# Gate and up of a SwiGLU layer as seven products of quarters, with DMAs that add in place

## The chip, the core and the metric

The kernel runs on one core of a Trainium2 chip. TensorE (PE) multiplies, VectorE (DVE) and ScalarE (ACT) work on tiles in on-chip memory, GpSimd (POOL) does some of the same work and issues DMAs, and SyncE (SP) issues most DMAs. The metric is the device time of one execution in microseconds (us).

## The reference

One step of a hybrid decoder layer on 512 prompt tokens and 8 sample tokens: parallel mLSTM and retention heads, cross attention into 256 memory tokens, and a dense SwiGLU layer. All that the change concerns is the last:

```python
D_MODEL = 1024; D_FF = 2816
...
hf = rmsnorm(x, g_ffn)
x = x + (jax.nn.silu(hf @ w_gate) * (hf @ w_up)) @ w_down
...
y = rmsnorm(x, g_final)
```

The arithmetic is fp32.

## The kernel before

**Data.** Activations lie transposed: 128 of the 1024 features on the partitions, eight such rows (`KB` = 8), and the N = 520 tokens in the free dimension, in two halves of H2 = 260. `X` holds the residual stream. An fp32 product is made of three matmuls of a rounded type: each operand is split into a high part (an ACT copy into the rounded type) and a low part (what is left, a DVE subtraction), and high·high, high·low and low·high are summed in PSUM. `split` (L179) does that for activations, `wload` (L188) for weights: SP loads 512 KB into one of three `wraw` tiles (L191), ACT casts (L195), DVE or at times POOL makes the low part (L196), in two pairs of tiles `whi`, `wlo`. `Weights` (L119) hands out the weights in a fixed order, one ahead of its use. `mm_k` (L206, matmul at L210) issues the six matmuls (128x128 by 128x260) of one row, `proj` (L234) the eight rows of one output block, 48 matmuls into a pair of PSUM banks, of which there are two (`ps2`).

**The stage.** The SwiGLU layer begins when the last rows of `A`, the split input times its gain, and the row factors `r_bc` (the norm's 1/rms, L262 to L265) are made. The 2816 hidden features are `FB` = 22 blocks of 128. For each block the loop at L1114 runs 48 matmuls for gate (`pfg`), takes them out of PSUM times `r_bc` (DVE, L1120), applies Silu (ACT, L1121), runs 48 matmuls for up (`pfu`), takes them out (DVE, L1124), multiplies (POOL, L1125) and splits the product into `FF` (L1126). Then come the eight output blocks of w_down (L1130 on), 22 rows of `FF` each, and the last of them in two halves of the tokens with the final norm and the stores behind (`finish`, L1143).

**Order.** The kernel is written against a tile framework (`tile.TileContext` with `schedule_with_timeline_sim=True`): a scheduler fixes ahead of time the order of the instructions on each engine, and each engine runs its list in order. Pools of rotating buffers (`bufs`) decide when a load may start.

Of the kernel before, what the change touches and what calls it, by code (L numbers as in the profile page):

```python
# [23 lines left out]
P = 128  # L24
# [66 lines left out]
def weight_order():  # L91
# [27 lines left out]
class Weights:  # L119


    def __init__(self, load, order):
        self.load, self.todo, self.ready, self.at = load, list(enumerate(order)), [], 0

    def get(self, ahead=1):
        while self.todo and len(self.ready) <= ahead:
            index, (_, _, nk, _, ncol) = self.todo.pop(0)
            self.ready.append(self.load(index, self.at, nk, ncol, len(self.todo) < 3))
            self.at += P * nk * ncol
        return self.ready.pop(0)  # L130
# [3 lines left out]
def decoder_step(ctx: ExitStack, tc: tile.TileContext, i: dict, o: list):  # L134
# [7 lines left out]
    apool_cm = tc.tile_pool(name="apool", bufs=1, side="right")  # L142
    apool = apool_cm.__enter__()
    bpool_cm = tc.tile_pool(name="bpool", bufs=1)
    bpool = bpool_cm.__enter__()
# [33 lines left out]
    def split(hi, lo, src, scale=None):  # L179
# [4 lines left out]
        else:  # L184
            act.activation(hi, src, AF.Copy, scale=scale)
            dve.scalar_tensor_tensor(lo, src, scale, hi.bitcast(F32), ALU.mult, ALU.subtract)

    def wload(index, at, nk, ncol, kept):  # L188
        n = nk * ncol
        raw = wp.tile([P, KB * P], F32, tag="wraw", name="wraw", bufs=3)  # L190
        sp.dma_start(raw[:, :n], i["weights"][at : at + P * n].rearrange("(p n) -> p n", p=P))  # L191
# [41 lines left out]

    def proj(x, name, order=range(KB)):  # L234
        hi, lo = W.get()
        ps = ps2(name)
# [61 lines left out]
    pool.memset(gw.bitcast(F32), 0.0)  # L298
    bg = main.tile([P, 8], F32, name="bg")
    m0 = main.tile([NS, 4], F32, name="m0")  # L300
    pool.dma_start(bg, i["b_gate"].broadcast_to([P, 8]))
# [808 lines left out]
    cx.close()  # L1110
    bpool_cm.__exit__(None, None, None)


    fx = ExitStack()  # L1114
    fp = fx.enter_context(tc.tile_pool(name="fp", bufs=2))
    FF = fp.tile([P, 2, FB, N], F32R, name="FF", bufs=1)
    for f in range(FB):
        ps = proj(A, "pfg")
        g = fp.tile([P, N], F32, tag="fg", name="fg")
        dve.tensor_tensor(halves(g), ps[:, :, :H2], r_h, ALU.mult)  # L1120
        act.activation(g, g, AF.Silu)  # L1121
        ps = proj(A, "pfu")
        u = fp.tile([P, N], F32, tag="fu", name="fu")
# [3 lines left out]
    apool_cm.__exit__(None, None, None)  # L1127
    tc.keep_in_program_order(act.preload_act_table_set(LOG_EXP))

    yx = ExitStack()  # L1130
    yp = yx.enter_context(tc.tile_pool(name="yp", bufs=4, side="right"))
    for ob in range(KB - 1):
        ps = ps2("pfd")
        for k0 in range(0, FB, KB):
            hi, lo = W.get()
            for k in range(min(KB, FB - k0)):
                mm_k(ps, hi, lo, FF, k, k0 + k, k0 + k == 0, k0 + k == FB - 1)
        xb = X[:, ob]
        dve.tensor_tensor(halves(xb), halves(xb), ps[:, :, :H2], ALU.add)
        square(yp, ob)  # L1140
        act.activation(xb, xb, AF.Copy, scale=vec[:, ob, V_GO : V_GO + 1])

    xb = X[:, KB - 1]  # L1143
    chunks = []
    def finish(ts, n, ps):
# [3 lines left out]
        dve.tensor_tensor(xb[:, ts], xb[:, ts], ps, ALU.add)  # L1149
        sq7 = yp.tile([P, n], F32, name="sq7")  # L1150
# [4 lines left out]
        r = yp.tile([P, n], F32, name="r")  # L1155
        rsqrt_rows(yp, r, pn)
# [90 lines left out]
```

## Time and profile before

| | before |
|---|---|
| median of 3 runs | 896.25 us (893.82 to 897.25) |
| the profiled execution's own time | 898.87 us |
| its span in the profile | 897.10 us |
| gate and up, first to last matmul | 499.9 to 756.65 us |
| w_down up to its last block | 756.65 to 867.55 us |
| PE busy | 863.6 us |
| DVE busy | 573.1 us |
| ACT busy | 349.7 us |
| POOL busy | 212.0 us |

The profile is of one execution. A busy time is that of an engine over the whole span. The chain of waits follows the work that ended last back from the end, at each step to what released it. In the timeline a bracket gives the idle time of the engine before an instruction and what ended it. Windows give the busy time of PE, its weight load, DVE, ACT and POOL in a stretch with the number of instructions in parentheses, then the granted TensorE clock (1.00 is full), the share of time that the DMA engines were busy, and GB/s. A DMA has two times: its issue on a queue and its landing.

### The profile page before, as it was taken

How to read it: one execution, taken by the hardware profiler on the slowest of the kernel's cores; microseconds unless marked ns; L12 is line 12 of the kernel's file. 1: busy time of each engine (PE TensorE's matmuls, PEld its weight loads, DVE VectorE, ACT ScalarE, POOL GpSimd, SP SyncE). 2: the span in 40 equal slices, each digit the busy share in tenths (PEclk: the TensorE clock that was granted, in tenths of full speed). 3: DMA queues.
4: the chain of work that ended last, by engine and by line, in shares of the span. 5: the costliest groups of instructions: out<-in, count | busy, mean ns of one | idle time of the engine just before them, and what ended most of it. 6: DMA issues, size and time to landing. Idle time of an engine off the chain costs nothing.

```text
span 897.1 us, 17057 instructions
## 1 busy us (share of the span) xinstructions
PE 863.6 (96%) x6923; PEld 846.3 (94%) x6923; DVE 573.1 (64%) x1251; ACT 349.7 (39%) x658; POOL 212.0 (24%) x210
## 2 busy tenths in 40 slices
PE   6999989999999999999999899999999999999994
PEld 5989989999999999889999899999999999999994
DVE  5899998877886678867888844444444444232224
ACT  5445525444545344365443432222222223222221
POOL 5554432221025201423323211111111111010011
PEclk9999989999999999999999999999999999999998
DMA  8323323333345347775663233333233332223213
GB/s 266 96 95 122 102 76 118 121 102 122 107 142 202 95 142 232 250 251 159 212 215 115 71 95 94 94 88 85 90 93 95 95 94 81 91 90 104 91 42 95
DMA packets 34599, 110.56 MB, mean 123 GB/s; under 512 B 4000, under 2 KB 8480, under 8 KB 34264
## 3 DMA queue, kind: packets, MB, share of 16 engines
q1 hardware_dynamic: 28752, 96.06, 34.8%
q0 software_dynamic: 3616, 12.34, 3.9%
q10 hardware_dynamic: 2152, 1.08, 0.5%
q8 instruction: 54, 0.88, 0.4%
q14 instruction: 25, 0.20, 0.1%
HBM read 100.38 MB, written 9.07 MB: 122 GB/s over the span
## 4 chain that ended last, share of the span: by engine, by line
PE 74%; DVE 15%; DMA 5%; issue 2%; ACT 2%; POOL 1%; SPq 0%; DVEq 0%; ACTq 0%; POOLq 0%
PE pfg L210 14%; PE pfu L210 14%; PE pfd L210 12%; PE pcq L210 4%; PE pwc L210 3%; PE ppl L210 3%; PE pgt L210 3%; PE pwo L210 3%; PE prp L210 3%; DVE cv L505 2%; DVE wlo L196 2%; PE pcv L210 1%; PE pfd L1171 1%; DMA Ss<-in_state_S_dram 1%; DMA X<-in_x_dram 1%
## 5 line engine op out<-in xcount | busy, mean ns | idle before, releaser
L195 ACT CAST whi<-wraw 128x1024 fp32r<-128x1024 f32 (+1 forms) x140 | 144.9, 1036 | 318.1 <-issue 113.5
L196 DVE TENSOR_TENSOR wlo<-wraw,whi 128x1024 fp32r<-128x1024 f32 (+1 forms) x121 | 176.8, 1462 | 81.2 <-ACT whi L195 79.1
L210 PE MATMUL pfg<-A,whi 128*128 128x260 f32 x704 | 114.3, 284 | 0.4 <-DVE fg L1120 0.4
L210 PE MATMUL pfu<-A,whi 128*128 128x260 f32 x704 | 113.6, 283 | 0.0
L210 PE MATMUL pfd<-FF,whi 128*128 128x260 f32 x616 | 99.0, 282 | 0.0
L210 PEld LDWEIGHTS pfg<-A,whi 128*128 128x128 f32 x704 | 97.8, 191 | 0.6 <-issue 0.6
L210 PEld LDWEIGHTS pfu<-A,whi 128*128 128x128 f32 x704 | 96.8, 188 | 0.1
L210 PEld LDWEIGHTS pfd<-FF,whi 128*128 128x128 f32 x616 | 84.6, 188 | 0.0
L1125 POOL TENSOR_TENSOR fu<-fu,fg 128x520 f32<-128x520 f32 x22 | 28.8, 1309 | 227.0 <-ACT whi L195 203.1
L210 PE MATMUL pfg<-A,wlo 128*128 128x260 f32 x352 | 71.4, 285 | 0.0
L210 PE MATMUL pfu<-A,wlo 128*128 128x260 f32 x352 | 71.1, 283 | 0.0
L1124 DVE TENSOR_TENSOR fu<-pfu,r_bc 128x520 f32<-128x520 f32 x22 | 15.4, 699 | 76.7 <-PE pfu L210 76.7
L210 PE MATMUL pfd<-FF,wlo 128*128 128x260 f32 x308 | 61.9, 282 | 0.0
L196 POOL TENSOR_TENSOR wlo<-wraw,whi 128x1024 fp32r<-128x1024 f32 x19 | 45.5, 2397 | 66.9 <-ACT whi L195 61.8
L289 POOL TENSOR_TENSOR ssq<-ssq,sq 128x520 f32<-128x520 f32 x18 | 29.3, 1630 | 125.6 <-ACT sq L288 120.4
L210 PEld LDWEIGHTS pfg<-A,wlo 128*128 128x128 f32 x352 | 54.8, 190 | 0.0
L210 PEld LDWEIGHTS pfu<-A,wlo 128*128 128x128 f32 x352 | 54.3, 188 | 0.0
L210 PE MATMUL pwc<-B,whi 128*128 128x260 f32 x256 | 43.9, 287 | 4.0 <-DVE X L278 3.0
L210 PE MATMUL ppl<-A,whi 128*128 128x260 f32 x256 | 47.0, 297 | 0.6 <-DVE up L497 0.6
L210 PEld LDWEIGHTS pfd<-FF,wlo 128*128 128x128 f32 x308 | 47.4, 188 | 0.0
L210 PE MATMUL pcv<-A,whi 128*128 128x260 f32 x256 | 45.8, 295 | 0.6 <-ACT whi L195 0.6
L210 PE MATMUL prp<-A,whi 128*128 128x260 f32 x256 | 44.3, 289 | 0.0
(382 smaller groups left out, 1972.3 us busy)
## 6 DMA issues: line engine op xcount, KB each, us to landing
wraw<-in_weights_dram SPq DMA_DIRECT2D x132, 512.0 KB, 3.6
kv<-in_cache_k_dram SPq DMA_DIRECT2D x16, 512.0 KB, 4.4
kv<-in_cache_v_dram SPq DMA_DIRECT2D x16, 512.0 KB, 4.5
wraw<-in_weights_dram SPq DMA_DIRECT2D x8, 384.0 KB, 3.1
X<-in_x_dram SPq DMA_DIRECT2D x2, 1040.0 KB, 6.2
Cs<-in_state_C_dram POOLq DMA_DIRECT2D x4, 512.0 KB, 5.1
out_dram<-Cs POOLq DMA_DIRECT2D x4, 512.0 KB, 3.2
Ss<-in_state_S_dram POOLq DMA_DIRECT2D x4, 512.0 KB, 4.4
```

What stands on the lines that cost most here:

```text
L195: act.copy(hi[:, :n], raw[:, :n])
L196: (pool if index in LO_ON_POOL else dve).tensor_tensor(lo[:, :n], raw[:, :n], hi[:, :n].bitcast(F32), ALU.subtract)
L210: pe.matmul(ps[:m, a, :H2], w[:, k, c0 : c0 + m], x[:, s, xk, a * H2 : (a + 1) * H2], start=first and w is hi and s == 0, stop=last and w ...
L289: (dve if ob == KB - 1 else pool).tensor_tensor(ssq, ssq, s, ALU.add)
L505: dve.scalar_tensor_tensor(cv[:, :LO], up[:, j : j + LO], wc(j), cv[:, :LO], ALU.mult, ALU.add)
L1124: dve.tensor_tensor(halves(u), ps[:, :, :H2], r_h, ALU.mult)
L1125: pool.tensor_tensor(u, u, g, ALU.mult)
L1171: pe.matmul(ps, w[:, k], FF[:, s, k0 + k, ts], start=k0 + k == 0 and w is hi and s == 0, stop=k0 + k == FB - 1 and w is lo,)
```

## The change

Gate and up of a hidden block are together a product of a 2x2 array of weight quarters (a11, a12: the two halves of a gate tile along the 1024 features; a21, a22: those of the up tile) with a 2x2 array of quarters of the input (b11, b21: first 260 tokens; b12, b22: the other 260). Eight quarter products give it; a scheme with sums ahead and behind (Winograd's form of Strassen's) gives it by seven. Blocks 0 to 2 (`PLAIN` = 3) stay as they were, blocks 3 to 21 take the seven products.

- `operands` makes the input once: X times gain times r in fp32 (`xn`), four sums, and seven splits into `TT`.
- `weight_operands` makes a block's weights one block ahead: both tiles g and u by SP, four sums s1 to s4, seven splits into rings of eight `qhi`, `qlo`. The sum s1 = a21 + a22 is made by two DMAs: SP loads the first half of u, then a DMA issued by POOL adds the second half in place.
- `neg_split` is the other way to split: ACT makes the high part and its negative, and a DMA issued by POOL adds the source to the negative. It makes the seven input operands and, in each block, a11, a12 and a22 (from DRAM); s1 to s4 keep `split`.
- The three banks' worth of products are summed on the way out of PSUM by DVE; Silu runs on the two gate halves; the product of gate and up moves from POOL to DVE and stays fp32 in `FR`. The rows of `FR` are split later: eight in blocks 3 to 10 into `A`, where the first eight rows of the hidden features then lie, fourteen during block 21 into `TT`.
- w_down's first two output blocks run together, rows 0 to 7 of both first.
- To make room, constants of the earlier stages move to a pool that ends before the layer.

The diff, cut to its core:

```diff
@@ -107,8 +108,8 @@
-    for ob in range(KB):
-        out += [("w_down", k0 * P, min(KB, FB - k0), ob * P, P) for k0 in range(0, FB, KB)]
+    for obs in ((0, 1), *((ob,) for ob in range(2, KB))):
+        out += [("w_down", k0 * P, min(KB, FB - k0), ob * P, P) for k0 in range(0, FB, KB) for ob in obs]
...
+    def neg_split(hi, lo, x, src):
+
+        act.copy(hi, x)
+        act.activation(lo, hi.bitcast(F32), AF.Copy, scale=-1.0)
+        pool.dma_start(lo, src, accum_op=ALU.add)
+
+    def operands():
+
+        for k in range(KB):
+            dve.scalar_tensor_tensor(xn[:, :, k], halves(X[:, k]), vec[:, k, V_GF : V_GF + 1], r_h, ALU.mult, ALU.mult)
+            if k % 2:
+                yield 1
+        b11, b21, b12, b22 = (xn[:, a, k : k + 4].rearrange("p k n -> p (k n)") for a in range(2) for k in (0, 4))
+        t3 = fr[:, 12 * N : 14 * N]
+        dve.tensor_tensor(t3, b22, b12, ALU.subtract)
+        dve.tensor_tensor(b12, b12, b11, ALU.subtract)
+        xsplit(0, b11)
+        yield 1
+        dve.tensor_tensor(b11, b22, b12, ALU.subtract)
+        xsplit(4, b21)
+        yield 1
+        dve.tensor_tensor(b21, b21, b11, ALU.subtract)
+        for j, x in ((1, t3), (6, b22), (3, b12), (2, b11), (5, b21)):
+            xsplit(j, x)
+            yield 1
+
+    def weight_operands(out):
+
+        at, at_u = W.next()[1], W.next()[1]
+        g, u = wraw(at, KB * P), wraw(at_u, KB * P)
...
+        s13, s24 = (wp.tile([P, KB * P], F32R, tag=t, name="wsum", bufs=2).bitcast(F32) for t in ("whi", "wlo"))
+        a11, a12, a21, a22, s3, s1, s2, s4 = (t[:, z : z + 4 * P] for t in (g, u, s13, s24) for z in (0, 4 * P))
+        sp.dma_start(s1, u_dram[:, : 4 * P])
+        pool.dma_start(s1, u_dram[:, 4 * P :], accum_op=ALU.add)
+        yield 1
+        dve.tensor_tensor(s3, a11, a21, ALU.subtract)
+        dve.tensor_tensor(s2, s1, a11, ALU.subtract)
+        dve.tensor_tensor(s4, a12, s2, ALU.subtract)
+        for w in (a11, s3, s2, s1, a12, a22, s4):
+            hi, lo = (tp.tile([P, 4 * P], F32R, tag="q" + t, name="q" + t, bufs=8) for t in ("hi", "lo"))
+            if w is a11 or w is a12 or w is a22:
+                neg_split(hi, lo, w, g_dram[:, : 4 * P] if w is a11 else g_dram[:, 4 * P :] if w is a12 else u_dram[:, 4 * P :])
+            else:
+                split(hi, lo, w)
+            out.append((hi, lo))
+            yield 1
...
+    spawn(operands())
+    ops = []
+    for f in range(PLAIN):
         ps = proj(A, "pfg")
...
-        pool.tensor_tensor(u, u, g, ALU.mult)
-        split(FF[:, 0, f], FF[:, 1, f], u)
...
+        dve.tensor_tensor(FR[:, f], u, g, ALU.mult)
+        step()
+    drain()
+    for f in range(PLAIN, FB):
...
+        for j, (out, (wh, wl), (xh, xl)) in enumerate(zip(ps, ops, xs)):
+            for k in range(4):
+                for w, x in ((wh, xh), (wh, xl), (wl, xh)):
+                    pe.matmul(
+                        out, w[:, k * P : (k + 1) * P], x[:, k * H2 : (k + 1) * H2],
+                        start=k == 0 and w is wh and x is xh, stop=k == 3 and w is wl,
+                    )
+            next(more, None)
+            if j == 0:
+                act.copy(g1, out)
+            elif j == 2:
+                dve.tensor_tensor(g2, out, g1, ALU.add)
+                dve.tensor_tensor(v1, ps[1], g2, ALU.add)
+            elif j == 3:
+                dve.tensor_tensor(gu[:, 1::2], out.unsqueeze(1).broadcast_to([P, 2, H2]), gu[:, 1:3], ALU.add)
+            elif j == 4:
+                dve.tensor_tensor(g1, out, g1, ALU.add)
+                act.activation(g1, g1, AF.Silu)
+            elif j == 6:
+                dve.tensor_tensor(gu[:, 1:3], cd[:, ::-1, :H2], gu[:, 1:3], ALU.add)
+                act.activation(g2, g2, AF.Silu)
+                to = FR[:, f - KB if f >= KB else f]
+                dve.tensor_tensor(halves(to), gu[:, 0:2], gu[:, 2:4], ALU.mult)
+            if f - PLAIN < KB and j == 5:
+                ff_split(f - PLAIN, FR[:, f - PLAIN])
+            if last:
+                if j == 1:
+                    W.fill(1)
+                for z in (2 * j, 2 * j + 1):
+                    ff_split(KB + z, FR[:, z])
```

The order of the instructions on every engine is the same in both kernels up to the SwiGLU layer. From there it moves. First DVE where the layer begins. `nrml` and `r_bc` are the norm, `pfg` and `pfu` the gate and up banks of blocks 0 and 1. Before:

```order
L264 SCALAR_TENSOR_TENSOR r_bc<-r_bc,nrmv 128x260 x2
L265 SCALAR_TENSOR_TENSOR r_bc<-r_bc,nrml 128x260 x2
L1120 TENSOR_TENSOR fg<-pfg,r_bc 128x520
L1124 TENSOR_TENSOR fu<-pfu,r_bc 128x520
L196 TENSOR_TENSOR wlo<-wraw,whi 128x1024
L183 TENSOR_TENSOR FF<-fu,FF 128x520
L1120 TENSOR_TENSOR fg<-pfg,r_bc 128x520
```

The change, on the same engine (the rows at L1158 are `xn`, those at L1163 to L1170 the sums of its quarters, L1206 and L1212 take out gate and up, L1213 is their product):

```order
L278 SCALAR_TENSOR_TENSOR r_bc<-r_bc,nrml 128x260 x2
L1158 SCALAR_TENSOR_TENSOR FR<-X,vec,r_bc 128x2x260 x6
L1206 TENSOR_TENSOR gu<-pfg,r_bc 128x520
L1158 SCALAR_TENSOR_TENSOR FR<-X,vec,r_bc 128x2x260 x2
L1212 TENSOR_TENSOR gu<-pfu,r_bc 128x520
L209 TENSOR_TENSOR wlo<-wraw,whi 128x1024
L1163 TENSOR_TENSOR FR<-FR 128x1040
L1213 TENSOR_TENSOR FR<-gu 128x520
L1164 TENSOR_TENSOR FR<-FR 128x1040
L1167 TENSOR_TENSOR FR<-FR 128x1040
L1170 TENSOR_TENSOR FR<-FR 128x1040
L1206 TENSOR_TENSOR gu<-pfg,r_bc 128x520
```

Six of the eight `xn` operations now stand ahead of emptying block 0's gate bank, and all four sums ahead of emptying block 1's.

Second, DVE in a block in the middle of the layer. Before:

```order
L1120 TENSOR_TENSOR fg<-pfg,r_bc 128x520
L196 TENSOR_TENSOR wlo<-wraw,whi 128x1024
L1124 TENSOR_TENSOR fu<-pfu,r_bc 128x520
L196 TENSOR_TENSOR wlo<-wraw,whi 128x1024
L183 TENSOR_TENSOR FF<-fu,FF 128x520
```

The change, one of the eight blocks that also split a hidden row (`wsum` 7453 holds s2 and s4 and 7452 s3 and s1 of the next block, 7309 and 7310 those of this one; `pfa` to `pfe` are product banks, `A_80` the split row):

```order
L1186 TENSOR_TENSOR wsum_7453<-wsum_7452,wraw_7448 128x512
L192 TENSOR_TENSOR A_80<-FR_6315,A_80 128x520
L1235 TENSOR_TENSOR gu_7318<-pfa_7313,gu_7318 128x260
L1187 TENSOR_TENSOR wsum_7453<-wraw_7448,wsum_7453 128x512
L192 TENSOR_TENSOR qlo_7387<-wsum_7309,qhi_7386 128x512
L1236 TENSOR_TENSOR gu_7318<-pfd_7316,gu_7318 128x260
L1240 TENSOR_TENSOR gu_7318<-pfe_7317,gu_7318 128x260
L1185 TENSOR_TENSOR wsum_7452<-wraw_7448,wraw_7450 128x512
L1238 TENSOR_TENSOR gu_7318<-pfa_7313,gu_7318 128x2x260
L192 TENSOR_TENSOR qlo_7442<-wsum_7310,qhi_7441 128x512
L1243 TENSOR_TENSOR gu_7318<-pfb_7314,gu_7318 128x520
```

The sum s2 of the next block, which reads the s1 that the two DMAs make, stands ahead of the adds of this block's products and of the low part of this block's s1 (qlo 7387).

Third, the queues that issue the weights, in the same stretch. SP before:

```order
L191 DMA wraw_6840<-in_weights_dram 128x1024
L191 DMA wraw_6900<-in_weights_dram 128x1024
L191 DMA wraw_6958<-in_weights_dram 128x1024
L191 DMA wraw_7018<-in_weights_dram 128x1024
L191 DMA wraw_7076<-in_weights_dram 128x1024
```

SP in the change (two `wraw` loads to a block are those of gate and up):

```order
L199 DMA wraw_7448<-in_weights_dram 128x1024
L199 DMA wraw_7450<-in_weights_dram 128x1024
L1182 DMA wsum_7595<-in_weights_dram 128x512
L199 DMA wraw_7591<-in_weights_dram 128x1024
L199 DMA wraw_7593<-in_weights_dram 128x1024
L1182 DMA wsum_7738<-in_weights_dram 128x512
```

The load of the next s1 stands on SP ahead of the next block's two weight loads. POOL, which issued no DMA here before but multiplied gate by up, has in the change:

```order
L1183 DMA wsum_7595<-in_weights_dram 128x512
L1153 DMA qlo_7478<-in_weights_dram 128x512
L1153 DMA qlo_7547<-in_weights_dram 128x512
L1153 DMA qlo_7566<-in_weights_dram 128x512
L1183 DMA wsum_7738<-in_weights_dram 128x512
```

Four adding DMAs a block now stand on POOL: one for s1, then those of a11, a12 and a22.

## Rows read from the trace of the kernel before

**Rows 1.** The page's first part: busy us, share of the span, instructions.

```profile
PE 863.6 (96%) x6923; PEld 846.3 (94%) x6923; DVE 573.1 (64%) x1251; ACT 349.7 (39%) x658; POOL 212.0 (24%) x210
```

**Rows 2.** The chain of waits: start, us, engine, operation, line, count.

```profile
514.24 5.98 PE pfg L210 x48
...
537.52 5.77 PE pfg L210 x48
...
750.88 5.77 PE pfu L210 x48
756.65 110.89 PE pfd L210 x924
867.55 7.96 PE pfd L1171 x66
```

**Rows 3.** A window of gate and up: PE, PEld, DVE, ACT, POOL, clock, DMA, GB/s.

```profile
566.35:750.00 183.65, 183.65 (x1531) 183.65 (x1530) 89.42 (x80) 52.09 (x64) 20.95 (x16) 1.00 0.31 91
```

**Rows 4.** Groups by shape: count, then busy us, mean ns, idle before and releaser.

```profile
L183 DVE TENSOR_TENSOR pT<-ppT,pT 128x512 fp32r<-128x512 f32 x8 | 5.3, 682 | 1.3 <-ACT pT L182 1.3
L495 DVE TENSOR_TENSOR up<-pcv,r_bc 128x260 f32<-128x260 f32 x8 | 3.3, 413 | 0.0
L1120 DVE TENSOR_TENSOR fg<-pfg,r_bc 128x520 f32<-128x520 f32 x22 | 15.4, 699 | 38.8 <-PE pfg L210 38.8
L182 ACT CAST B<-qf 128x512 fp32r<-128x512 f32 x8 | 4.8, 616 | 1.6 <-DVE qf L1060 1.6
L262 ACT ACTIVATE nrml<-nrml 128x260 f32<-128x260 f32 x7 | 3.0, 422 | 0.2
```

**Rows 5.** Timeline: start, us, engine, line, operation, count, idle before and releaser.

```profile
498.12 0.75 DVE L186 SCALAR_TENSOR_TENSOR A<-X,vec,A 128x520 fp32r<-128x520 f32 x1
498.25 0.74 PE L210 MATMUL pwc<-B,whi 128*128 128x260 f32 x4 [2.70 <-DVE X L278]
498.79 0.68 DVE L278 TENSOR_TENSOR X<-X,pwc 128x520 f32<-128x520 f32 x1
...
513.39 0.70 DVE L1120 TENSOR_TENSOR fg<-pfg,r_bc 128x520 f32<-128x520 f32 x1
513.65 1.05 ACT L195 CAST whi<-wraw 128x1024 fp32r<-128x1024 f32 x1 [2.57 <-PE pfu L210]
514.00 0.69 DVE L1124 TENSOR_TENSOR fu<-pfu,r_bc 128x520 f32<-128x520 f32 x1
...
514.72 1.28 ACT L1121 ACT_TABLE_LOAD   x1
...
567.28 1.23 DVE L196 TENSOR_TENSOR wlo<-wraw,whi 128x1024 fp32r<-128x1024 f32 x1 [0.19 <-ACT whi L195]
...
573.04 2.37 DVE L196 TENSOR_TENSOR wlo<-wraw,whi 128x1024 fp32r<-128x1024 f32 x1 [0.19 <-ACT whi L195]
```

**Rows 6.** DMA issues of the run: queue, count, KB each, us to landing.

```profile
wraw<-in_weights_dram SPq DMA_DIRECT2D x132, 512.0 KB, 3.6
...
Cs<-in_state_C_dram POOLq DMA_DIRECT2D x4, 512.0 KB, 5.1
...
out_dram<-vf POOLq DMA_DIRECT2D x4, 256.0 KB, 5.1
...
X<-in_x_dram SPq DMA_DIRECT2D x2, 260.0 KB, 3.0
...
cosr<-in_rope_dram POOLq DMA_DIRECT2D x1, 260.0 KB, 3.0
```

**Rows 7.** Windows at the start of the layer, columns as in rows 3.

```profile
500.00:502.00 2.00, 2.00 (x11) 2.00 (x11) 1.96 (x4) 2.00 (x4) 1.92 (x2) 0.50 0.03 8
502.00:504.00 2.00, 2.00 (x15) 2.00 (x15) 2.00 (x1) 0.86 (x2) 1.03 (x1) 0.75 0.00 0
```

**Rows 8.** DMA issues of the window from 420 to 480 us, columns as in rows 6.

```profile
wraw<-in_weights_dram SPq DMA_DIRECT2D x6, 512.0 KB, 4.4
```

**Rows 9.** A window at the start of the kernel, columns as in rows 3.

```profile
0.00:20.00 20.00, 11.85 (x54) 9.80 (x55) 10.71 (x13) 12.67 (x19) 12.76 (x21) 1.00 0.90 295
```

More of the change, by code (lines that the diff above doesn't have):

```diff
@@ L36 @@
 FB = DFF // P
+PLAIN = 3
 EPS = 1e-6
@@ L123, in __init__, with next, fill @@
         self.load, self.todo, self.ready, self.at = load, list(enumerate(order)), [], 0
+    def next(self):
+        index, (_, _, nk, _, ncol) = self.todo.pop(0)
+        at, self.at = self.at, self.at + P * nk * ncol
+        return index, at, nk, ncol, len(self.todo) < 3
+    def fill(self, ahead):
+        while self.todo and len(self.ready) <= ahead:
+            self.ready.append(self.load(*self.next()))
     def get(self, ahead=1):
[L126 to L129, printed above, removed]
+        self.fill(ahead)
         return self.ready.pop(0)
@@ L143, in decoder_step @@
     apool = apool_cm.__enter__()
+    ctab_cm = tc.tile_pool(name="ctab", bufs=1)
+    ctab = ctab_cm.__enter__()
     bpool_cm = tc.tile_pool(name="bpool", bufs=1)
@@ L232, in drain, with proj @@
             step()
-    def proj(x, name, order=range(KB)):
-        hi, lo = W.get()
+    def proj(x, name, order=range(KB), ahead=1):
+        hi, lo = W.get(ahead)
         ps = ps2(name)
@@ L1111, in decoder_step @@
     bpool_cm.__exit__(None, None, None)
+    ctab_cm.__exit__(None, None, None)
+    eps_c = vec[:, 0, V_BUF : V_BUF + 1]
+    dve.memset(eps_c, EPS)
     fx = ExitStack()
-    fp = fx.enter_context(tc.tile_pool(name="fp", bufs=2))
-    FF = fp.tile([P, 2, FB, N], F32R, name="FF", bufs=1)
-    for f in range(FB):
+    fp = fx.enter_context(tc.tile_pool(name="fp", bufs=1))
+    TT = fp.tile([P, FB - KB, 2, N], F32R, name="TT")
+    FR = fp.tile([P, FB - KB, N], F32, name="FR")
+    tp_cm = tc.tile_pool(name="tp", bufs=2)
@@ new lines, in decoder_step, with ff, xsplit @@
+    tp = tp_cm.__enter__()
+    Q = 4 * H2
+    tt, fr = TT.rearrange("p b s n -> p (b s n)"), FR.rearrange("p b n -> p (b n)")
+    xs = [(tt[:, 2 * j * Q : (2 * j + 1) * Q], tt[:, (2 * j + 1) * Q : 2 * (j + 1) * Q]) for j in range(7)]
+    xn = fr[:, 4 * N : 12 * N].rearrange("p (a k n) -> p a k n", a=2, k=KB)
+    def ff(s, k, ts):
+        return A[:, s, k, ts] if k < KB else TT[:, k - KB, s, ts]
+    def xsplit(j, x):
+        neg_split(*xs[j], x, x)
+    def neg_split(hi, lo, x, src):
+        act.copy(hi, x)
+        act.activation(lo, hi.bitcast(F32), AF.Copy, scale=-1.0)
+        pool.dma_start(lo, src, accum_op=ALU.add)
@@ L1123, in decoder_step @@
-        u = fp.tile([P, N], F32, tag="fu", name="fu")
+        if f == PLAIN - 1:
+            spawn(weight_operands(ops))
+        step()
+        ps = proj(A, "pfu", ahead=int(f < PLAIN - 1))
         dve.tensor_tensor(halves(u), ps[:, :, :H2], r_h, ALU.mult)
-        pool.tensor_tensor(u, u, g, ALU.mult)
-        split(FF[:, 0, f], FF[:, 1, f], u)
-    apool_cm.__exit__(None, None, None)
+        dve.tensor_tensor(FR[:, f], u, g, ALU.mult)
+        step()
+    drain()
+    for f in range(PLAIN, FB):
+        last, nxt = f == FB - 1, []
+        more = weight_operands(nxt) if not last else iter(())
+        next(more, None)
+        ab, cd = ps2("pfa"), ps2("pfb")
+        ps = [*(ps1(z)[:, :H2] for z in ("pfc", "pfd")), ab[:, 0, :H2], ab[:, 1, :H2], ps1("pfe")[:, :H2], cd[:, 0, :H2], cd[:, 1, :H2]]
+        gu = tp.tile([P, 4, H2], F32, tag="gu", name="gu")
+        g1, g2, v1, v2 = (gu[:, z] for z in range(4))
+        for j, (out, (wh, wl), (xh, xl)) in enumerate(zip(ps, ops, xs)):
[5 more added lines that the diff above has]
+                    )
+            next(more, None)
+            if j == 0:
[20 more added lines that the diff above has]
+                    ff_split(KB + z, FR[:, z])
+        list(more)
+        ops = nxt
@@ L1128, in decoder_step @@
+    tp_cm.__exit__(None, None, None)
     tc.keep_in_program_order(act.preload_act_table_set(LOG_EXP))
     yx = ExitStack()
-    yp = yx.enter_context(tc.tile_pool(name="yp", bufs=4, side="right"))
-    for ob in range(KB - 1):
-        ps = ps2("pfd")
+    yp = yx.enter_context(tc.tile_pool(name="yp", bufs=4))
+    for obs in ((0, 1), *((ob,) for ob in range(2, KB - 1))):
+        pss = [ps2("pfd") for _ in obs]
         for k0 in range(0, FB, KB):
[L1135 to L1141, printed above, removed]
+            for ps in pss:
+                hi, lo = W.get()
+                for k in range(k0, min(k0 + KB, FB)):
+                    for w, s in ((hi, 0), (hi, 1), (lo, 0)):
+                        for a in range(2):
+                            pe.matmul(
+                                ps[:, a, :H2], w[:, k - k0], ff(s, k, slice(a * H2, (a + 1) * H2)),
+                                start=k == 0 and w is hi and s == 0, stop=k == FB - 1 and w is lo,
+                            )
+        for ob, ps in zip(obs, pss):
+            xb = X[:, ob]
+            dve.tensor_tensor(halves(xb), halves(xb), ps[:, :, :H2], ALU.add)
+            square(yp, ob)
+            act.activation(xb, xb, AF.Copy, scale=vec[:, ob, V_GO : V_GO + 1])
@@ L1183, in decoder_step @@
     fx.close()
+    apool_cm.__exit__(None, None, None)
 _INS = ["b_gate", "state_mlstm_n", "state_mlstm_m"]
```

30 lines of the change are left out of this document (18 added, 12 removed).

## Prediction

> **What bounds the kernel now.** I read the page's busy shares first, then the chain of waits, then the stage that the change touches. The page has PE busy 96% of the span, DVE 64%, ACT 39%, POOL 24% [rows 1]. The chain shows what that means in the gate and up stage: from 514.24 to 756.65 us it is PE alone, stretches of 48 matmuls of 5.77 us, gate and up in turn, nothing between them; then w_down, 924 matmuls in 110.89 us [rows 2]. So one matmul of 260 columns costs 5.767/48 = 0.1201 us a block of 96 costs 11.53 us, and blocks 3 to 21 take 537.52 to 756.65, 219.1 us. In the same stage DVE is busy 89.4 of 183.65 us, ACT 52.1, POOL 21.0, the DMA engines 0.31 of the time at 91 GB/s, at full granted clock [rows 3]. PE's count of matmuls bounds the stage; the others are about half idle.
>
> **What the change takes away.** A product block has 7 x 4 x 3 = 84 matmuls of the same shape for 96. Twelve in a row now go to one bank where two halves alternated; the last output block of w_down already does that, 66 in 7.96 us, 0.1206 each [rows 2], so the pace stays. 19 blocks x 12 x 0.1201 = **-27.4 us**; a product block costs 10.09 us of PE. Up to the gate and up stage the order on all five engines is the old one, so nothing before about 498 us moves.
>
> **What it adds, engine by engine.** Per product block DVE has three differences and four low parts of 128x512 (0.68 each), three adds of 260 columns (0.41), and three operations of 520 (0.70); for eight blocks one low part of a hidden row more (0.70) [rows 4]. That is 4.8 + 1.2 + 2.1 = 8.1 to 8.8 us of 10.09, and a little less since such operations start 0.61 apart (513.39 and 514.00 in rows 5). The old slowdown of DVE beside POOL's product (2.37 us at 573.04 for a low part that took 1.23 at 567.28) [rows 5] goes, as that product moves to DVE. ACT has ten passes of 512 (0.62), a copy and two Silu halves (0.42 each by a row of that size) and at times a cast (0.62): 7.4 to 8.1 us [rows 4]. POOL only issues four DMAs. By sums nobody passes PE. By waits somebody may.
>
> **The start, +14.6 us.** (a) DVE now does six of the eight new products of X ahead of emptying block 0's gate bank, and PE needs that bank for block 1. Before, DVE empties it at 513.39 and PE goes on at 514.24; with a vector scalar one such step takes 0.67 (498.12 to 498.79) [rows 5]: 6 x 0.67 = +4.0, PE resumes at 518.2 and ends block 1 at 529.8. (b) Ahead of emptying block 1's gate bank DVE has the difference that overwrites a quarter of X, and that waits for the adding DMA which reads it. ACT reaches that operand's second pass late: two passes of 1.05, table load 1.28 [rows 5], a Silu of 0.6, two passes, one more, about 523.5; a DMA issued by POOL with 512 KB lands 5.1 later [rows 6]; difference 1.2, emptying 0.7: 530.6. Block 2's gate weights are cast by ACT after four more passes, near 532, and then PE stands at a low part of the first product whose DMA lands near 533.5. Less what PE can do between: +2.9. (c) PE's clock. In this trace PE waited 2.70 us before 498.25, and then the granted clock was 0.50 from 500 to 502 and 0.75 to 504, the lower of its two levels (1.2 GHz) for about 3 us: 1.5 us lost [rows 5, 7]. Two holds of this size: +3.0. (d) The buffer for the first block's sum is that of block 2's gate weights, so load (3.4), add (4.4), difference, cast and low part (2.0) begin when that gate ends: 9.8 us, beside 5.77 + 1.44 of PE work: +2.6; the fifth product's add, behind five ACT passes, +2.1. Each can be off by half: 8 to 20 together. Should DVE do the X products as early as the r rows stand and nothing else wait, (a) remains.
>
> **The steady blocks, +6.2 us.** Each block's sum s1 is loaded by SP, and a second DMA, issued by POOL, adds the other half of u to it in place. Two buffers rotate, so the load waits until DVE has made the low part of the s1 before the last. In DVE's order this makes a ring: low part of s1, load, adding DMA, difference s2 of the block after the next, an add of product 3, low part of a hidden row (eight blocks), difference s4, low part of the next s1. DVE's part is 0.61 x 3 + 0.41 + 0.68 + hand-overs 0.1 = 3.0 us, 2.4 without the hidden row. The ring must turn within 10.09. The load: 260 KB land after 3.0 [rows 6]; 512 KB after 3.6 over the run but 4.4 in the stretch where most is loaded [rows 8], so 3.0 to 3.8, I take 3.4. The adding DMA is in no row: below stands a 260 KB load issued by POOL, 3.0, above it a 256 KB store issued by POOL, 5.1 [rows 6]; I take 4.4, nearer to the upper because it reads its destination too. The ring is then 10.8 us in the 7 steady blocks with a hidden row and 10.2 in the other 11: 187.8 for 18 x 10.09 = 181.6, +6.2. At 3.0 and 3.0 it is 9.0 and hidden (0); at 3.8 and 5.1 it is 11.9 and 11.3: +26.
>
> The Trainium skill, "Collectives: The Full Stack", section "The bandwidth ceiling: the fold count and why AG ≠ RS ≠ AR", says that a reducing DMA is slower than a copy because it needs two source reads, at about half the rate. By it the four adds of a block would hold the engines like eight copies, which is the third rival's size; no run here shows it yet.
>
> The other ring, weights of u (load 3.6, 4.4 when busy) to difference s3, its cast, and six ACT passes to the cast that frees the buffer, is 3.6 + 5.4 = 9.0 to 9.9 us, inside the block by 0.2 to 1.1. The eight-deep ring of operands gives the other three adds about a block.
>
> **The end, +1.** In the last block ACT and DVE split fourteen hidden rows, 14 x 0.70 = 9.8 us of DVE beside 10.09 of PE; w_down's first two output blocks now take rows 0 to 7 first, 2 x 48 x 0.12 = 11.5 us of cover. I take 1, between 0 and 3. Without that cover it would be some 8.
>
> **Sum.** -27.4 + 14.6 + 6.2 + 1.0 = -5.6 on the profiled execution's 898.87 (span 897.10): 893.3. That execution lies 2.62 above the median 896.25 of the three runs, so 890.7 as a median. What a measurement of this kernel can tell from no change is about 0.5%, 4.5 us.
>
> **Rivals.**
> *The DMAs stay hidden* (0.24). POOL's loads of 260 KB land in 3.0, and at 0.31 the engines are idle [rows 3, 6]. Ring 9.0, steady term 0: 898.87 - 27.4 + 14.6 + 1 = 887.1, 884.5 as a median, 878 if the start costs 8.
> *The ring of s1 is slow, and the kernel slower* (0.20). Place: DVE's difference s2, which stands ahead of four operations that PE waits for. At 3.8 + 5.1 the term is 26: 913, 910 as a median. It decides from load + add = 8.1 us on: 27.4 - 14.6 - 1 = 11.8 us over 18 blocks, 0.66 each on 10.09, less 2.6 of DVE (mean). The rows for it are the busy landings [rows 8] and the store's 5.1; against it, the s1 load meets only half an engine's load.
> *The DMA engines become the bound* (0.13). 1 MB in 11.53 us at a share of 0.31 is 3.4 us of all engines per MB (91/0.31 = 294 GB/s at full share) [rows 3]. A block now moves 2.36 MB by copies and adds, 8.0 us; if an add holds the engines twice, 3.41 MB, 11.6 us a block: 18 x 1.5 = +27, so 914, 911 as a median. Against it: at a share of 0.90 they moved 295 GB/s, 328 at full share [rows 9], so 10.4 us.
> *The matmuls saved were not the bound* (0.05): no change, 896. The chain without a gap speaks against it [rows 2].
>
> **How the numbers follow.** The forecast has 0.38, the rivals 0.62. A gain over 4.5 us: 0.21 of the forecast's 0.38 (its centre lies just past the line, and the start alone can move it 6 either way) and the hidden case's 0.24: 0.45. Within: 0.13 of the forecast, the last rival, 0.05 of the slow ring: 0.23. Slower: 0.04 + 0.15 + 0.13 = 0.32. Cases of both signs hold most of it; the forecast's own range is 884 to 898. The whole range reaches from the hidden case with a cheap start, 877, to the two slow ones, 912.
>
> **What would show it.** Right: product blocks of 10.1 to 10.8 us, PE's short waits in them for a low part or a sum; the adding DMA 4 to 5 us from issue to landing; a gap of 4 us on PE near 514 behind the products of X, and half clock after it. Hidden case: 10.09 a block, DVE waiting for PE. Slow ring: DVE idle ahead of s2 for the adding DMA in each block. DMA bound: share above 0.9 through the stage. Wrong from the ground: matmuls of the products slower than 0.120, or a stage before 498 that moved.

## The result and the profile after

The changed kernel took 932.21 us (median of four, 931.08 to 935.08) beside 895.23 us for the kernel before on the same chip: a ratio of 1.0416, 95% interval 1.0381 to 1.0451. It is 37 us slower, where 5.6 us faster was forecast, and 20 us beyond the upper end of the range. The profiled execution took 935.08 us, with a span of 933.30.

Where the time went is seen from three places in the two traces: the first matmul of the gate, the first one of w_down, and the end.

| us | before | after |
|---|---|---|
| gate and up: first gate matmul to first w_down matmul | 256.5 | 293.8 |
| w_down, norm and stores, to the end of the span | 140.6 | 142.0 |

All but 1.4 us of the loss lies in the stage that was to gain. Its matmuls are worth 226.3 us now (3 x 96 + 19 x 84 of them at 0.1201), so 67 us of it are lost, where the kernel before lost 3.

First the engines and the two large DMA queues, from the page of after (q1 carries SP's loads, q0 what POOL issues: packets, MB, share of the time of all 16 DMA engines). PE's busy time fell by 9.6 us against [rows 1], its share from 96 to 91%:

```profile
PE 854.0 (91%) x6695; PEld 831.3 (89%) x6695; DVE 629.1 (67%) x1438; ACT 442.0 (47%) x862; POOL 255.9 (27%) x271
...
q1 hardware_dynamic: 31488, 101.04, 33.6%
q0 software_dynamic: 15568, 35.99, 19.1%
```

The same queue on the page of the kernel before:

```profile
q0 software_dynamic: 3616, 12.34, 3.9%
```

POOL's queue held the DMA engines for 35.0 us of 897.1 before and for 178.3 us of 933.3 now, 143 us for 23.65 MB more.

The windows of the stage (columns as in [rows 3]: PE, its weight load, DVE, ACT, POOL, clock, DMA share, GB/s). In [rows 3] PE had no idle time, the clock was 1.00 and the DMA share 0.31. Now PE stands 21 of 150 us, runs part of the rest at the lower level, and the DMA share is 0.83:

```profile
498.00:560.00 62.00, 46.81 (x345) 45.28 (x344) 37.47 (x54) 34.05 (x47) 14.14 (x15) 0.92 0.64 152
...
600.00:750.00 150.00, 128.96 (x982) 125.92 (x982) 87.43 (x154) 82.69 (x156) 40.60 (x46) 0.94 0.83 185
```

The chain of waits, which in [rows 2] was PE alone through the stage, now runs from DMA to DMA:

```profile
642.75 4.45 DMA wsum<-in_weights_dram
647.20 0.02 issue
647.22 0.69 DVE wsum L1186
647.91 0.34 DVE gu L1235
648.25 0.61 DVE qlo L192
648.86 0.02 issue
648.88 5.25 DMA wsum<-in_weights_dram
...
654.69 0.49 POOL wsum L1183
...
655.23 6.88 DMA qlo<-in_weights_dram
662.10 0.04 issue
662.15 2.33 PE pfb L1227 x9
```

At 642.75 the second half of u is added to s1, at 647.22 DVE makes s2, at 648.25 the low part of the older s1, and only then is the next s1 loaded. That is the ring that the prediction drew, and it closes in nearly every block. From 600 to 735 us, some ten and a half blocks, DVE stood nine times ahead of s2 for the adding DMA (us, times, longest):

```profile
DVE wsum L1186 <- DMA wsum<-in_weights_dram: 23.4, 9, 5.7
```

SP issued the loads of s1 from 598.64 to 737.32 us in eleven turns of 12.61 us. In the chain from 600 to 750 us the two DMAs of s1 are 61% of the time, those of the low parts 5%. Behind the ring stands a wait that the prediction took for covered: the low part of a weight quarter, 6.88 us from issue to landing, for which PE waits. Its DMA was issued right behind the add of s1 (654.69), which POOL had held until s1's load landed. The product blocks tell the sum: the first matmul of a product stands at 599.72 in one block and at 765.34 thirteen blocks later, 12.74 us a block for 10.09 of matmuls.

```profile
599.72 0.41 PE L1227 MATMUL pfc<-TT,qhi 128*128 128x260 f32 x2
...
765.34 0.41 PE L1227 MATMUL pfc<-TT,qhi 128*128 128x260 f32 x2
```

### The profile page after: what moved, and what is told of

Its sections match the earlier page's. It is cut to its first block, busy times and chain, and to the rows that moved or that the text cites. A ratio compares the mean times of both kernels' runs of the same rounds, so it can differ in the third digit from the quotient of the medians.

```text
span 933.3 us, 17322 instructions
## 1 busy us (share of the span) xinstructions
PE 854.0 (91%) x6695; PEld 831.3 (89%) x6695; DVE 629.1 (67%) x1438; ACT 442.0 (47%) x862; POOL 255.9 (27%) x271
## 4 chain that ended last, share of the span: by engine, by line
PE 54%; DMA 21%; DVE 18%; issue 3%; ACT 3%; POOL 1%; SPq 0%; DVEq 0%; POOLq 0%; ACTq 0%
DMA wsum<-in_weights_dram 13%; PE pfd L1269 12%; PE pgt L223 5%; PE pcq L223 5%; PE pwo L223 5%; PE pwc L223 3%; PE ppl L223 3%; DMA qlo<-in_weights_dram 3%; PE prp L223 3%; DMA wraw<-in_weights_dram 2%; DVE cv L518 2%; DVE wlo L209 2%; PE pcv L223 1%; DVE qlo L192 1%; PE pfg L223 1%
## 5 line engine op out<-in xcount | busy, mean ns | idle before, releaser
L209 DVE TENSOR_TENSOR wlo<-wraw,whi 128x1024 fp32r<-128x1024 f32 (+1 forms) x83 | 107.9, 1303 | 74.9 <-ACT whi L208 73.0
L1153 POOL DMA_DIRECT2D qlo<-in_weights_dram x57 | 55.2, 1034 | 95.6 <-ACT qlo L1152 86.5
L1227 PE MATMUL pfa<-TT,qhi 128*128 128x260 f32 x304 | 58.7, 290 | 11.8 <-DVE gu L1235 9.1
L191 ACT CAST qhi<-wsum 128x512 fp32r<-128x512 f32 x76 | 46.1, 616 | 49.1 <-DVE wsum L1185 21.1
L1227 PE MATMUL pfb<-TT,qhi 128*128 128x260 f32 x304 | 62.0, 297 | 1.5 <-DVE gu L1243 1.4
L1269 PE MATMUL pfd<-TT,whi 128*128 128x260 f32 x392 | 62.8, 282 | 0.0
L1227 PEld LDWEIGHTS pfa<-TT,qhi 128*128 128x128 f32 x304 | 47.9, 193 | 13.7 <-DVE gu L1235 10.9
L192 DVE TENSOR_TENSOR qlo<-wsum,qhi 128x512 fp32r<-128x512 f32 x76 | 52.0, 687 | 9.7 <-ACT qhi L191 8.9
L1269 PEld LDWEIGHTS pfd<-TT,whi 128*128 128x128 f32 x392 | 53.7, 188 | 0.0
L1227 PEld LDWEIGHTS pfb<-TT,qhi 128*128 128x128 f32 x304 | 51.0, 202 | 2.2 <-ACT gu L1233 1.9
```

Of the source, the lines that this page charges most:

```text
L191: act.copy(hi, src)
L192: dve.tensor_tensor(lo, src, hi.bitcast(F32), ALU.subtract)
L1153: pool.dma_start(lo, src, accum_op=ALU.add)
L1227: pe.matmul(out, w[:, k * P : (k + 1) * P], x[:, k * H2 : (k + 1) * H2], start=k == 0 and w is wh and x is xh, stop=k == 3 and w is wl,)
L1269: pe.matmul(ps[:, a, :H2], w[:, k - k0], ff(s, k, slice(a * H2, (a + 1) * H2)), start=k == 0 and w is hi and s == 0, stop=k == FB - 1 and ...
```

## Experiments

Each is the changed kernel with one or a few edits, run beside the kernel before, which took 893.2 to 894.5 us in these comparisons. "Stage" is the length of gate and up as in the table above.

### Which of the four adding DMAs, and what in it: the order kept, adds made copies

Three kernels keep every instruction and every DMA of the changed kernel in its place, and only let a DMA copy where it added. Their low parts, or s1, are then not the reference's.

```diff
-        pool.dma_start(lo, src, accum_op=ALU.add)
+        pool.dma_start(lo, src, accum_op=ALU.add if lo.shape[-1] == Q else ALU.bypass)   # e3_copy_a, e12_copy_all_w
...
-        pool.dma_start(s1, u_dram[:, 4 * P :], accum_op=ALU.add)
+        pool.dma_start(s1, u_dram[:, 4 * P :])   # e4_copy_s1, e12_copy_all_w
```

> The DMAs for the low parts of a11, a12 and a22 copy instead of adding (the products' low parts are then not the reference's); order and number of instructions and DMAs unchanged, the s1 pair untouched. If the s1 ring is slow by itself, with landing times that do not depend on the other DMAs: blocks stay at 12.5 to 12.8 us, 928 to 934 us. If the adding DMAs hold the engines longer than copies and so make every landing late: engine time per block falls by three times 0.74 us, s1's load lands in about 3.6 and its add in about 3.7, blocks of 10.1 to 11.2, 887 to 910 us.

> Only s1's second DMA copies instead of adding (s1 is then not the reference's); order and number of instructions and DMAs unchanged. Ring theory: the ring loses what an add costs over a copy, some 0.7 to 1.0 us of 12.74, so 914 to 920 us. If adding costs nothing over copying from issue to landing: 930 to 934 us.

> The order of the changed kernel without an edit; all four DMAs of a product block that add to weights copy instead (the products are then not the reference's). Copying three saved 27 us, copying the one of s1 17. If the hold of the engines is the cause and the two savings add: 887 to 891 us. If POOL's queue, where s1's DMA waits for its load ahead of the others, or s1's ring keeps a part: 896 to 904 us.

Measured: 904.84 us (stage 267.2) with the three low parts copied, 916.16 us (stage 276.0) with s1 copied, 898.07 us (stage 260.5) with all four copied, ratio of the last to the kernel before 1.0032 (1.0012 to 1.0052). So 34 us of the changed kernel's time are the difference between adding and copying. With the 27.4 us of matmuls saved, 64 us had been lost; the other 30 have other causes. The two savings, 27 and 16, add to 43 and not to 34, so they overlap.

With the low parts copied the time lies in the case in which adds make every landing late, with s1 copied in the case of the ring theory (914 to 920), and with all four copied in the case in which the ring or POOL's queue keeps a part. All three are understood when the four kernels are put beside each other. Landings are the medians on the pages; a turn is the mean from one load of s1 to the next on SP, over eleven turns between 598 and 738 us.

| us | s1's load | s1's second DMA | both | a turn of the ring |
|---|---|---|---|---|
| the changed kernel | 5.3 | 4.4 | 9.7 | 12.61 |
| e4_copy_s1 | 5.5 | 3.3 | 8.8 | 11.42 |
| e3_copy_a | 4.0 | 4.2 | 8.2 | 10.99 |
| e12_copy_all_w | 4.0 | 3.5 | 7.5 | 10.63 |

The turn is the two landings and 2.6 to 3.1 us more each time, near the prediction's 2.4 to 3.0 for DVE and a hand-over on POOL that it left out. So in this order of instructions the ring of s1 sets the block, and the three other adds, which are no part of it, lengthen it by making its load land later: 4.0 us when they copy, 5.3 when they add.

The page of e12_copy_all_w has the price of adding on its queue:

```profile
q0 software_dynamic: 14352, 35.99, 13.7%
...
qlo<-in_weights_dram POOLq DMA_DIRECT2D x57, 256.0 KB, 4.2
```

And the page of the changed kernel:

```profile
qlo<-in_weights_dram POOLq DMA_DIRECT2D x57, 256.0 KB, 6.5
...
wsum<-in_weights_dram SPq DMA_DIRECT2D x19, 256.0 KB, 5.3
wsum<-in_weights_dram POOLq DMA_DIRECT2D x19, 256.0 KB, 4.4
TT<-FR POOLq DMA_DIRECT2D x7, 520.0 KB, 7.8
```

The same 36 MB on the same queue took 123.1 us of the engines (13.7% of 898.3) instead of 178.3, 0.73 us less for each of the 76 DMAs. With the price of X's seven adds (19.3 us, from e5_x_split below) taken off, an adding DMA of 256 KB holds all 16 engines for about (178.3 - 19.3 - 35.0)/76 = 1.63 us, a copying one for (123.1 - 19.3 - 35.0)/76 = 0.91. The ratio is 1.8. That is near what the Trainium skill says in "Collectives: The Full Stack", section "The bandwidth ceiling: the fold count and why AG ≠ RS ≠ AR", of the reducing DMAs of a ring between ranks, that an add needs two source reads and so runs at half the rate of a copy; this case's rows agree to a tenth, on a transfer that is no collective.

The edit takes a second, smaller thing away. The instruction that issues the DMA occupies POOL longer when it adds (us in all, mean ns; the changed kernel, then e12_copy_all_w):

```profile
L1153 POOL DMA_DIRECT2D qlo<-in_weights_dram x57 | 55.2, 1034 | 95.6 <-ACT qlo L1152 86.5
L1153 POOL DMA_DIRECT2D qlo<-in_weights_dram x57 | 30.4, 535 | 103.6 <-ACT qlo L1152 98.4
```

That is at most 0.5 us of the 2.3 by which these landings shortened. No run separates it from the longer hold of the engines.

### Is it the ring of s1?

s1 takes turns in three places instead of two, so that its load waits for the sum three blocks back. The scheduler made the order of the engines anew for this edit, so more than the ring changed; the second kernel has the order of the first.

```diff
+        turn[0] += 1
+        s1 = (r_bc[:, : 4 * P], ssq[:, : 4 * P], s1)[turn[0] % 3]
```

> The same DMAs as the changed kernel, but s1 rotates over three places (two idle row tiles and its old one), so its load waits for the sum three blocks back. Ring theory: blocks fall from 12.74 to 10.1 to 10.6 us, 885 to 900 us in all. Engine theory: a block still holds the engines 10.6 us (0.83 of 12.74), landings get longer as the engines fill; blocks no shorter than 11.3, 905 to 930 us, DMA share above 0.93.

> Both edits at once: s1 rotates over three places as in e2_ring3, and the DMAs of a11, a12 and a22 copy instead of adding as in e3_copy_a (their low parts are then not the reference's). Alone the first gave 5 us of 932 and the second 27, to 10.99 us a block. If what is left of e3_copy_a's blocks over 10.09 is s1's ring, and the ring only matters once the engines are free: blocks of 10.1 to 10.4 us, 888 to 898 us. If the engines alone set the block: no gain over e3_copy_a, 901 to 906 us.

Measured: 927.32 us (stage 287.5), and 904.51 us (stage 266.3) with the three low parts copied as well, where copying alone gave 904.84 (267.2). The edit with its order is worth 5 us of 932 by itself and nothing with the engines freer. Neither theory comes out whole: the times are those of the engine theory, but its share above 0.93 was not reached. What the longer ring changed is in the DMA rows of e2_ring3 from 600 to 735 us (queue, count, KB, us to landing; `r_bc`, `ssq` and `wsum` are the three places), its window, and DVE's wait ahead of s2 there:

```profile
qlo<-in_weights_dram POOLq DMA_DIRECT2D x31, 256.0 KB, 7.2
r_bc<-in_weights_dram SPq DMA_DIRECT2D x4, 256.0 KB, 5.0
wsum<-in_weights_dram SPq DMA_DIRECT2D x4, 256.0 KB, 8.4
r_bc<-in_weights_dram POOLq DMA_DIRECT2D x4, 256.0 KB, 5.9
wsum<-in_weights_dram POOLq DMA_DIRECT2D x4, 256.0 KB, 6.2
ssq<-in_weights_dram SPq DMA_DIRECT2D x4, 256.0 KB, 4.7
ssq<-in_weights_dram POOLq DMA_DIRECT2D x4, 256.0 KB, 6.8
```

```profile
600.00:735.00 135.00, 118.93 (x917) 115.03 (x917) 80.89 (x144) 76.73 (x143) 37.56 (x43) 0.96 0.85 197
```

```profile
DVE wsum L1190 <- DMA wsum<-in_weights_dram: 23.5, 4, 9.2
```

The adds of s1 land later, after 5.9 to 6.8 us where they took 4.4, and the low parts after 7.2 instead of 6.5; the engines' share went only from 0.83 to 0.85. DVE waits for s1 in one block of three, where s1 is at its old place, but as long in all as the changed kernel in all its blocks (23.5 us to 23.4). The other blocks wait for low parts and weights instead, and the mean block, by the 917 matmuls of the window, is 12.4 us. So this pair does not decide against the ring: it shows that other chains through a landing stand close behind it.

### Taking the DMAs away

```diff
-        sp.dma_start(s1, u_dram[:, : 4 * P])
-        pool.dma_start(s1, u_dram[:, 4 * P :], accum_op=ALU.add)
         yield 1
+        dve.tensor_tensor(s1, a21, a22, ALU.add)   # e1, e11, e6 and later
...
-        neg_split(*xs[j], x, x)
+        split(*xs[j], x)   # e5, e6 and e7
...
-            if w is a11 or w is a12 or w is a22:
+            if False:   # e6 and later: split for all seven
```

> The sum s1 is made by DVE from the two halves of u on the chip; its load and its adding DMA go, all else stays. In the changed kernel 13 steady blocks take 12.74 us each, the chain runs through the load of s1 (5.3 us to landing) and the adding DMA (4.4), and the DMA engines are busy 0.83 of the time. Ring theory (the wait of s1's load for the low part two sums back sets the block): the ring is gone, blocks of 10.1 to 10.5, 885 to 897 us in all. Engine theory (the DMA engines are the bound): engine time per block falls from 10.6 to about 8.2 us, so 10.1 to 10.5 as well. Third theory (the ring of three weight tiles and the late low parts are as slow as s1 was): blocks of 11.3 or more, 905 us or more.

> As e1_s1_dve (s1 by DVE, no DMA for it), and the three DMAs left in a block copy instead of adding (low parts of a11, a12, a22 are then not the reference's); the order of all instructions is that of e1_s1_dve. If what the adds cost in e1_s1_dve's blocks (11.7 us) is the longer hold of the engines by an add: blocks of 10.1 to 10.4, 884 to 892 us. If it is the detour over POOL's queue and a landing, adding or not: blocks stay above 11.2, 904 us or more.

> Only the seven operands of X get their low parts from DVE instead of from ACT's negative and an adding DMA; the weights keep theirs. In the changed kernel the first block's low part of a11 lands 7.2 us after its issue, behind the seven adds of X, PE waits 3.41 us for it at 532 and then runs at the lower clock for about 4 us. If the adds of X are what the start loses beyond the 4.4 us at 514: 5 to 9 us less, 923 to 928 us. If the start waits as long for s1's two DMAs anyway: 929 to 934 us.

> No adding DMA at all: s1 and every low part are made by DVE; the only DMAs of a block are the two weight loads, as in the kernel before. DVE then has 18 operations in a block, at 0.6 us apart for the wide ones about 9.5 us, 10.1 with a hidden row. If the adding DMAs made all of the loss in the steady blocks: blocks of 10.1 to 10.4 us and 876 to 886 us in all, faster than before by 1 to 2%. If DVE becomes the bound in their place: blocks of 10.6 to 11.3 us, 890 to 902 us.

Measured: 912.50 us for s1 by DVE (stage 277.8), of the three cases in its expectation the third. The order of the engines is a new one here too, but there is no ring of s1 left, and its blocks, by the 859 matmuls of the window below, are 11.7 us instead of 12.7. With its three low parts copied instead of added, in the same order, 890.99 us (stage 246.7), so the adds alone cost that kernel 21 us, and the detour over POOL's queue does not. With only X's operands by DVE, 924.54 us (stage 285.8): X's adds are 8 us of the start. With no adding DMA, 886.79 us (stage 246.1), ratio to the kernel before 0.9927 (0.9899 to 0.9954): its blocks are those of its first case, its time is 0.8 us beyond it. Windows from 600 to 720 us; of e1_s1_dve:

```profile
600.00:720.00 120.00, 106.98 (x859) 104.90 (x858) 80.26 (x143) 72.14 (x134) 27.28 (x32) 0.99 0.71 158
```

of e11_s1_dve_copy_a:

```profile
600.00:720.00 120.00, 119.84 (x996) 119.42 (x995) 92.88 (x168) 82.21 (x155) 18.99 (x36) 1.00 0.61 181
```

of e12_copy_all_w:

```profile
600.00:720.00 120.00, 116.45 (x945) 114.22 (x945) 83.00 (x150) 75.49 (x147) 23.09 (x44) 1.00 0.74 221
```

of e6_no_add:

```profile
600.00:720.00 120.00, 120.00 (x999) 119.92 (x998) 114.27 (x204) 59.56 (x120) 0.00 (x0) 1.00 0.32 103
```

PE stands 13 us of 120 with three adds and no s1 DMA, although the engines are busy only 0.71 of the time, and hardly at all with three copies at 0.61. So the engines need not be full to cost time: a DMA that holds them longer lands later, and so does what is in flight beside it. From 600 to 720 us the low parts took 6.3 us from issue to landing in e1_s1_dve and 3.8 in e11_s1_dve_copy_a, and the weight loads, which are the same in both, 5.8 and 4.3. In e6_no_add PE has no gap, and ten blocks take 101.1 us, from a first product at 602.18 to the one at 703.30. DVE is busy 114 of 120 us there and still hides: the operations start 0.6 us apart.

### The start and the end

e7_no_add_late asks for the products of X only after block 0's gate bank is emptied. e9_end_late also puts the splits of the fourteen late hidden rows behind the last block's sums on DVE, beside w_down. e10_x_mixed gives four of X's seven operands back to adding DMAs, at the start alone, where DVE is full and the DMA engines are not.

```diff
-    spawn(operands())
...
+        if f == 0:
+            spawn(operands())   # in the loop of the plain blocks, behind Silu: e7, e9, e10
...
-                for z in (2 * j, 2 * j + 1):
-                    ff_split(KB + z, FR[:, z])
...
+    for z in range(FB - KB):   # behind the product blocks, in program order: e9, e10
+        hi, lo, raw = ff(0, KB + z, slice(None)), ff(1, KB + z, slice(None)), FR[:, z]
+        act.copy(hi, raw)
+        tc.keep_in_program_order(dve.tensor_tensor(lo, raw, hi.bitcast(F32), ALU.subtract))
...
-        neg_split(*xs[j], x, x)
+        (neg_split(*xs[j], x, x) if j in (2, 3, 5, 6) else split(*xs[j], x))   # e10
```

> As e6_no_add, and the eight products of X are asked for after block 0's gate bank is emptied, not before. If the six products ahead of that bank cost what the gap at 514 shows, 4.4 us and the 2 us of lower clock behind it: 5 to 7 us under e6_no_add. If PE then waits as long for the first operands: the same within 1.5 us.

> As e7_no_add_late, and the fourteen hidden rows are split behind the last block's sums on DVE, beside w_down's first two output blocks, instead of among them. In e7_no_add_late PE waits 6.15 us ahead of w_down for DVE to empty the last product's bank, and then runs about 6 us at the lower clock. If that wait is what the end costs: 6 to 9 us less, 876 to 880 us. If the rows then come too late for w_down's second third: 881 us or more.

> As e9_end_late, but four of the seven operands of X (products 2, 3, 5 and 6) get their low parts by adding DMAs, which takes 4.6 us of DVE's work out of the start, where DVE is busy without a gap. If DVE bounds the start: 1 to 4 us under e9_end_late. If the adds of 520 KB land too late (7 us or more): 1 to 4 us above it.

Measured: 885.10 us for e7_no_add_late (stage 243.9). That is neither of its two cases. The wait of 4.4 us at the first gate bank went, but only 2.2 us of the stage with it, and the 1.7 us between the medians are within what the runs scatter: DVE was busy 57 of the 62 us from 498 to 560, and PE met the same work later as waits of 0.3 to 0.8 us. e9_end_late: 874.83 us (stage 236.4), 10 us less where 6 to 9 were expected, 7.5 of them in the stage, where PE's wait ahead of w_down shrank. In e7_no_add_late:

```profile
744.82 1.20 PE L1269 MATMUL pfd<-A,whi 128*128 128x260 f32 x4 [6.15 <-DVE gu L1238]
```

and in e9_end_late:

```profile
731.40 0.75 PE L1271 MATMUL pfd<-A,whi 128*128 128x260 f32 x4 [0.79 <-DVE gu L1238]
```

The first four matmuls took 1.20 us against 0.75: the granted clock was 0.50, the lower of its two levels, from 744.8 to 748 us in e7_no_add_late, and 1.00 behind 731.4 in e9_end_late. e10_x_mixed: 870.81 us (stage 235.6), ratio to the kernel before 0.9751 (0.9710 to 0.9792), against 0.9775 (0.9748 to 0.9802) for e9_end_late. The two are not told apart. Both beat both kernels: seven products pay by 2.2 to 2.5% once no weight goes through an adding DMA and DVE's last splits stand behind its sums.

## Why the prediction was wrong, point by point

**The matmuls saved: right.** 27.4 us was taken off at the old pace, and e6_no_add shows it: PE without a gap at 10.11 us a block.

**The start, +14.6: right as a sum.** From 498 to 560 us PE stands 15.2 us and loses some 3 to the clock; the kernel before lost some 2.4 in that stretch. The first two parts came as drawn, and so did the two holds of the clock. PE's waits in the trace of after:

```profile
514.43 1.21 PE L223 MATMUL pfg<-A,whi 128*128 128x260 f32 x4 [4.42 <-DVE gu L1206]
...
532.25 0.46 PE L1227 MATMUL pfc<-TT,qlo 128*128 128x260 f32 x1 [3.41 <-DMA qlo<-in_weights_dram]
...
662.15 0.59 PE L1227 MATMUL pfb<-TT,qlo 128*128 128x260 f32 x1 [4.17 <-DMA qlo<-in_weights_dram]
...
791.31 0.77 PE L1269 MATMUL pfd<-A,whi 128*128 128x260 f32 x4 [3.22 <-DVE gu L1238]
```

4.42 us for the six products of X (4.0 were set), and the first low part landed at 532.2 (533.5). From 545 to 560 us, where the prediction's last part had 4.7, PE stood 7.4. The difference that overwrites a quarter of X did wait for the DMA that reads it, 4.50 us on DVE:

```profile
526.05 1.24 DVE L1170 TENSOR_TENSOR FR<-FR 128x1040 f32<-128x1040 f32 x1 [4.50 <-DMA TT<-FR]
```

**The steady blocks, +6.2: this is the step that failed.** Thirteen blocks of 12.74 us are 34 us above their matmuls by themselves, and the stage's balance leaves some 45 for all of it (37.3 + 27.4 less some 16 at the start and 3 at the end). The mechanism was right: the ring of s1 turns as drawn, and the sign that the prediction gave for it, DVE idle ahead of s2 for the adding DMA, stands in the trace nine times in ten and a half blocks. Two things in the step were wrong.

The first is the price of the ring's landings. The load of s1 was set at 3.4 and took 5.3; the adding DMA was set at 4.4 and took 4.4; the hand-over on POOL, 0.56 us between the load's landing (654.13) and the add's issue (654.69), was left out. The ring then turns in about 12.7 us without a hidden row, beyond the upper bound of 11.9. The prices were landings of single DMAs of the kernel before, whose engines were busy 0.31 of the time in this stage. With the three other adds beside it the share was 0.83, and when those adds copied, the same load in the same place took 4.0.

The second is that the other three adds were taken for covered, "about a block" by the eight-deep ring of operands, and given no price, neither of their own nor in the ring. Copying in their place gave 27 us. They land 6.5 us after their issue, and PE waited for them by name more than for anything else. With the ring of s1 gone (e1_s1_dve) the blocks still take 11.7 us. Among the products' matmuls of after:

```profile
  DMA qlo<-in_weights_dram: 20.1, 11
  DVE gu L1235: 9.1, 6
  ACT qhi L191: 6.1, 2
```

(us, times.) The rival "the DMA engines become the bound" had the price nearly right: 8.0 us of engine time a block by copies (e12_copy_all_w: a share of 0.74 over blocks of 10.6 us, so 7.9), 11.6 if an add counts twice, 10.4 at the faster rate (0.83 of 12.74 us is 10.6). It was wrong in its form. It asked for a share above 0.9 and for blocks as long as the engine time; the share is 0.83, and the blocks are 2 us longer than that. The rival "the ring of s1 is slow" had the place, the sign and the direction, and a sum of landings (8.9) nearer to the measured 9.7 than the forecast's 7.8. What neither had is the tie between them: the longer hold of the engines stretches the landings of s1's load, of the low parts and of the weights, and the ring carries the first of these into every block.

**The end, +1: mis-sized.** w_down's first two outputs cover the late rows, as said. But the splits of those rows stand on DVE among the sums that empty the last product banks, and w_down needs those banks. PE waited 3.22 us at 791.31, and the rest of the program took 1.4 us longer: 4.6. In e7_no_add_late, where DVE has more to do, the same wait is 6.15.

**The chances.** Slower had 0.32, and the range ended at 912 because each of the two slow rivals was priced alone. They share the DMA engines, so they came together, and the bound had to be taken with both.

**What stays open.** With all four DMAs copying, the stage is still 14 us longer than with s1 by DVE and three copies (260.5 against 246.7). In the steady blocks, 10.6 us against 10.1, the trace of e12_copy_all_w names the ring of s1: 4.0 and 3.6 us for the two DMAs from 644 us on, 10.51 us from one load to the next. The rest lies at the start and the end, where the two kernels' orders also differ. In the changed kernel the add of s1 also holds POOL while it waits for its load, ahead of the low part of a11, and s1's load stands on SP ahead of the next weights. No run here gives these two a price, and none lengthens the ring with the order kept.

## What to carry to other kernels

A transfer that adds in place is no free use of an idle queue: count it on the DMA engines at nearly twice a copy, and add up all DMAs of one turn of the loop before any chain through a landing is priced, since landings read beside few other DMAs did not hold beside many here. A ring through two landings passes every lengthening on to each turn. When several suspects share a resource, their upper bounds belong together in the range. An experiment that keeps every instruction in place and only turns the add into a copy tells the price of the add from that of the wait; one that changes the order with it, as the longer ring did, tells less.

## What was not expected of the hardware

An adding DMA of 256 KB took about 1.63 us of all 16 engines, a copy of the same size by the same queue 0.91, and its instruction held POOL for 0.87 us instead of 0.53. PE lost 13 of 120 us to landings at a DMA share of 0.71, and next to nothing at 0.61. With a longer ring of buffers the adding DMA of s1 landed in 5.9 to 6.8 us instead of 4.4, and the block was hardly shorter. DVE could be busy 114 of 120 us without a wait of PE for it.
